# Row maxima of the grouped-query heads: both heads of a block side by side in the two halves of the array's rows

## Chip, core and metric

One core of a Trainium2 chip runs the whole program. The metric is the device time of one execution in microseconds (us). TensorE is PE in the rows (its weight loads are PEld), VectorE is DVE, ScalarE is ACT, GpSimd is POOL, and SyncE, which issues the transfers, is SP.

## The reference, cut to what matters

A trunk of two layers over 1024 latent tokens and 256 context tokens. Layer 0 has two kinds of attention over 1280 keys: differential attention, and grouped-query attention with 8 query heads of 64 columns, four to each of 2 key heads. The change touches only the second kind:

```python
def gqa_attention(q, k, v):
    q = q.reshape(bsz, nq, B_KV_HEADS, B_REP, HEAD_DIM)
    s = jnp.einsum('bqgrd,bkgd->bgrqk', q, k) * (HEAD_DIM ** -0.5)
    p = jax.nn.softmax(s.astype(jnp.float32), axis=-1).astype(v.dtype)
    o = jnp.einsum('bgrqk,bkgd->bqgrd', p, v)
```

The softmax stays the same whatever is subtracted from the scores of a query, so long as the exponentials stay in range. The kernel subtracts the largest score over the keys, found ahead of time.

## The kernel before

The kernel is built with a tile framework: the program issues operations in its own order, a scheduler orders them on each engine by its own costs and by priorities (`tc.high_priority`), and each engine then runs its list strictly in that order.

The class `Grouped` handles the grouped heads after the differential ones. The work is cut into 8 blocks `j`, each with 512 queries of two heads (`s` = 0 and 1). `prepare` brings the queries of a block to 64 rows of head dimension. Each float32 value is split into a rounded high part and the rest, the low part. For head `s` the tile `q[s]` holds the high part in rows 64s to 64s+63 and the low part in the other 64 rows. The keys lie in three groups of 512, 512 and 256 (`GROUPS`); `k1` holds the keys' high part twice, in both halves of the rows.

Per block there are ten steps `kt`, one for each 128 keys. In a step `exponentials` computes the scores of 128 keys by 512 queries for either head, with two matmuls that add up in one PSUM bank (L1433, L1434), and ACT writes the exponential to `pt` (L1435). POOL or DVE adds `pt` to a running sum (L1439). Two steps later `values` multiplies `pt` by the values (L1448). The values of one head are 64 columns wide, so that the two heads use the two halves of the array's columns: `tile_position=(0, s * 64)`. These are two instructions, one for each half of the columns. `divide` (L1463 to L1470) does the normalisation of a block.

The shift of the next block is found at the same time. In each of the steps 0 to 7, `ahead` calls `maximum` for 128 queries of one head: three matmuls of all 128 rows (L1407, into three banks), one DVE maximum of each bank (L1409), and one more of the three results (L1410), whose negative goes to `w`. At step 8 `shifts` turns `w` around (L1416) and puts it into the tile `q2`, which the matmul L1434 applies. `first` does the same for block 0, during the last steps of the differential attention (L1324 and L1202 are its values and its transposes there).

All these scores, for exponentials and for maxima, come from one pool of five PSUM banks (`bank`).

Of the kernel before, what the change touches and what calls it, by code (L numbers as in the profile page):

```python
# [9 lines left out]
F32 = mybir.dt.float32  # L10
# [3 lines left out]
AX = mybir.AxisListType  # L14
PSUM = bass.MemoryType.PSUM

P = 128
# [38 lines left out]
class Trunk:  # L56
# [838 lines left out]
    def merged(self, w, bs, k0, mod, gcol, step):  # L895
# [88 lines left out]
        for n in range(2):  # L984
            ahead(n)
        yield
        for n in range(len(seq)):
            if n + 2 < len(seq):
                ahead(n + 2)
            x, p = seq[n]  # L990
            on = x in (6, 7, 4, 3)
            if p == 0:
                ps[x] = ps[{6: 1, 7: 6, 4: 7, 3: 5}[x]] if on else [self.ps() for _ in range(4)]
            if p == 6 and x in (1, 6, 7, 4):
                for j in range(4):
                    jj, h = {1: (j, 0), 6: (j, 1), 7: (4 + j, 1), 4: (4 + j, 0)}[x]
                    self.tc.keep_in_program_order(self.residual(jj, self.acc[jj, h]))
            a, b = parts.pop((x, p)), bparts.pop((x, p))
            for j in range(4):
                f = slice(j * P, (j + 1) * P)  # L1000
                self.mm3(ps[x][j], a[0][:, f], a[1][:, f], *b, p == 0 and not on, p == pairs[-1], skip_group_check=on)
            if p == pairs[-1]:
                with self.tc.high_priority(offset=60):
                    plus(x)
            step(x, p)
# [33 lines left out]
    def conv(self):  # L1039
# [49 lines left out]
        for h in range(2):  # L1089
            if h == 1:  # L1090
                parts = self.blocks([self.cw_in[17], self.cw_in[1]])
            for i, x in enumerate((8, 16, 0, 9)):
                first(x, h)
                if h == 1:
                    if x == 16:
                        z[0, "y"] = convolve(0, [z[8, i] for i in range(2)])
                        y = z[0, "y"]
                        times(y[0], z[0, 0], y[0])
                        self.leave(y[0], 0, 0)
                    self.combine(i)  # L1100
# [243 lines left out]
class Grouped:  # L1344
# [52 lines left out]
            nc.vector.scalar_tensor_tensor(out=q[s][o, :], in0=tr[r, :], scalar=0.125,  # L1397
                                           in1=q[s][r, :].bitcast(F32), op0=ALU.mult, op1=ALU.subtract)

    def maximum(self, j, i, s):  # L1400

        nc = self.nc
        c = 64 - s * 64
        mx = self.at.pl.tile([P, 4], F32, name="mx3", bufs=4)
        for g, ((g0, gn), (k1, _)) in enumerate(zip(GROUPS, self.k[j // 4])):
            o = self.bank()
            nc.tensor.matmul(o[:, 0:gn * P], lhsT=self.q[j][s][:, i * P:(i + 1) * P], rhs=k1[:, 0:gn * P], start=True,  # L1407
                             stop=True)
            nc.vector.reduce_max(out=mx[:, g:g + 1], in_=o[:, 0:gn * P], axis=AX.X)  # L1409
        nc.vector.reduce_max(out=self.w[j % 2][:, i, c:c + 1], in_=mx[:, 0:3], axis=AX.X, negate=True)  # L1410

    def shifts(self, j):
        nc = self.nc
# [57 lines left out]

    def first(self, k):
        with self.t.tc.high_priority(offset=60):
            for m in range(k * 4, min(8, k * 4 + 4)):
                self.maximum(0, m // 2, m % 2)
            if k == 1:
                self.shifts(0)
        if k == 1:
            self.prepare(1)
# [18 lines left out]

    def ahead(self, j, m):
        with self.t.tc.high_priority(offset=40):  # L1500
            if m < 8:
                self.maximum(j, m // 2, m % 2)
            if m == 8:
                self.shifts(j)

# [57 lines left out]
```

## Time and profile before

| | |
|---|---|
| median of 3 runs (lowest to highest) | 2538.68 us (2537.96 to 2540.46) |
| profiled execution, its own time | 2539.14 us |
| its span from the first instruction to the last | 2537.3 us |
| granted TensorE clock, mean | 0.989 of full speed |
| share of the span in which PE, DVE, ACT, POOL are busy | 96%, 73%, 48%, 12% |

The time of the profiled execution is 1.8 us above its span and 0.5 us above the median. The grouped heads lie between 511 and 751 us of the span, the maxima of block 0 between 494 and 511 us.

### The profile page before, as it was taken

What the parts mean: (1) busy time and instruction counts of PE and PEld (TensorE: products, weight loads), DVE (VectorE), ACT (ScalarE), POOL (GpSimd) and SP (SyncE); (2) the same over time, 40 slices, a digit from 0 to 9 for tenths busy, and PEclk for the clock granted to TensorE, in tenths of its full rate; (3) what the DMA queues carried; (4) which work ended last, traced back from release to release, by engine and by line L of the source; (5) the groups of instructions that cost most, each with busy time, mean ns of one, the idle gap of its engine ahead of it and who ended that gap; (6) DMA issues with size and microseconds to landing.
All of it is one profiled execution on the core that took longest, in us unless ns stands there. A gap on an engine that the chain in (4) does not pass through costs nothing.

```text
span 2537.3 us, 30356 instructions
## 1 busy us (share of the span) xinstructions
PE 2437.0 (96%) x11070; PEld 1902.7 (75%) x11070; DVE 1861.5 (73%) x2903; ACT 1226.4 (48%) x1986; POOL 297.5 (12%) x201
## 2 busy tenths in 40 slices
PE   7999899999999999999999998999999999999997
PEld 5888677744448778777788877887877888878886
DVE  4857888887867887776857688766788556585766
ACT  3113578755552465444444446533246555545443
POOL 0001000044440420000000033001131000000011
PEclk9999999999999999999999999999999999999999
DMA  7811111000011047778642320223203444853231
GB/s 271 282 61 51 22 23 46 7 25 6 1 65 68 1 154 239 254 252 302 242 150 92 109 89 31 68 76 127 92 30 105 163 142 152 295 186 133 100 108 67
DMA packets 118519, 297.15 MB, mean 117 GB/s; under 512 B 13536, under 2 KB 19296, under 8 KB 118368
## 3 DMA queue, kind: packets, MB, share of 16 engines
q1 hardware_dynamic: 118368, 295.20, 34.2%
q8 instruction: 87, 1.43, 0.2%
q14 instruction: 64, 0.52, 0.1%
HBM read 225.29 MB, written 63.96 MB: 114 GB/s over the span
## 4 chain that ended last, share of the span: by engine, by line
PE 65%; DVE 19%; ACT 6%; DMA 6%; issue 3%; SPq 0%; POOL 0%; ACTq 0%; DVEq 0%; POOLq 0%
PE ps L75 17%; PE ps L74 17%; PE ps L76 17%; PE pv L1448 3%; DMA raw<-in_w 3%; PE one L1324 2%; PE s L1433 2%; DVE acc L675 1%; PE s L1407 1%; PE s L1434 1%; PE s L1187 1%; DMA xr<-in_xT 1%; ACT e L1193 1%; DVE mx L1409 1%; DVE a L79 1%
## 5 line engine op out<-in xcount | busy, mean ns | idle before, releaser
L74 PE MATMUL ps<-bh,part 128*128 128x512 f32 x784 | 306.7, 392 | 7.7 <-ACT part L940 7.5
L75 PE MATMUL ps<-bl,part 128*128 128x512 f32 x784 | 305.1, 390 | 0.0
L76 PE MATMUL ps<-bh,part 128*128 128x512 f32 x784 | 303.3, 391 | 0.0
L940 ACT CAST part<-a 128x512 fp32r<-128x512 f32 x196 | 121.5, 622 | 270.7 <-PE ps L75 129.8
L74 PE MATMUL ps<-T,a 128*128 128x512 f32 x608 | 240.5, 396 | 10.3 <-ACT tmp L882 4.1
L75 PE MATMUL ps<-T,a 128*128 128x512 f32 x608 | 238.5, 392 | 1.6 <-DVE T L79 1.6
L76 PE MATMUL ps<-T,a 128*128 128x512 f32 x608 | 238.0, 392 | 0.0
L79 DVE TENSOR_TENSOR part<-a,part 128x512 fp32r<-128x512 f32 x196 | 135.1, 691 | 130.6 <-ACT part L940 129.9
L79 DVE TENSOR_TENSOR a<-raw,a 128x1024 fp32r<-128x1024 f32 (+1 forms) x114 | 121.6, 1068 | 98.8 <-PE ps L75 68.4
L79 POOL TENSOR_TENSOR hid<-graw,hid 128x512 fp32r<-128x512 f32 x24 | 38.0, 1607 | 1258.1 <-ACT hid L538 1258.0
L74 PEld LDWEIGHTS ps<-bh,part 128*128 128x128 f32 x784 | 147.1, 188 | 42.9 <-ACT part L940 13.0
L74 PE MATMUL ps<-H,a 128*128 128x512 f32 x456 | 177.8, 390 | 0.0
L75 PE MATMUL ps<-H,a 128*128 128x512 f32 x456 | 177.6, 389 | 0.0
L76 PE MATMUL ps<-H,a 128*128 128x512 f32 x456 | 177.3, 389 | 0.0
L76 PEld LDWEIGHTS ps<-bh,part 128*128 128x128 f32 x784 | 147.1, 188 | 33.2 <-DVE part L79 2.6
L75 PEld LDWEIGHTS ps<-bl,part 128*128 128x128 f32 x784 | 147.1, 188 | 30.1 <-DVE bl L79 0.4
L538 ACT CAST a<-raw 128x1024 fp32r<-128x1024 f32 (+1 forms) x114 | 101.4, 906 | 136.0 <-PE ps L75 78.5
L858 DVE TENSOR_TENSOR tmp<-ps,tmp 128x512 f32<-128x512 f32 x114 | 78.5, 688 | 109.7 <-PE ps L76 73.5
L74 PEld LDWEIGHTS ps<-T,a 128*128 128x128 f32 x608 | 114.6, 188 | 42.9 <-ACT tmp L882 7.6
L79 DVE TENSOR_TENSOR bl<-b,bh 128x1024 fp32r<-128x1024 f32 x98 | 119.9, 1223 | 22.3 <-ACT bh L927 22.0
L75 PEld LDWEIGHTS ps<-T,a 128*128 128x128 f32 x608 | 114.7, 189 | 25.9 <-DVE T L79 2.9
L76 PEld LDWEIGHTS ps<-T,a 128*128 128x128 f32 x608 | 114.9, 189 | 24.1
(417 smaller groups left out, 5864.8 us busy)
## 6 DMA issues: line engine op xcount, KB each, us to landing
gq<-tmp SPq DMA_DIRECT2D x196, 256.0 KB, 3.3
b<-gq SPq DMA_DIRECT2D x98, 512.0 KB, 3.2
raw<-in_w SPq DMA_DIRECT2D x72, 512.0 KB, 4.5
a<-in_w SPq DMA_DIRECT2D x140, 256.0 KB, 5.6
raw<-in_adaT SPq DMA_DIRECT2D x48, 512.0 KB, 5.9
adar<-in_adaT SPq DMA_DIRECT2D x32, 512.0 KB, 5.0
raw<-in_cw_in SPq DMA_DIRECT2D x24, 512.0 KB, 3.7
ada<-in_adaN SPq DMA_DIRECT2D x16, 512.0 KB, 8.4
```

The lines of the kernel that those rows point to most:

```text
L74: mm(ps, lhsT=lh, rhs=rh, start=start, stop=False, **kw)
L75: mm(ps, lhsT=lh, rhs=rl, start=False, stop=False, **kw)
L76: mm(ps, lhsT=ll, rhs=rh, start=False, stop=stop, **kw)
L79: return eng.tensor_tensor(out=out, in0=a, in1=hi.bitcast(F32), op=ALU.subtract)
L538: self.nc.scalar.copy(out=hi, in_=src)
L675: self.eng(L("mul")[j]).tensor_tensor(out=acc, in0=acc, in1=y, op=ALU.mult)
L858: nc.vector.tensor_tensor(out=o, in0=a, in1=b, op=op)
L940: self.tc.keep_in_program_order(nc.scalar.copy(out=hi, in_=src))
L1187: nc.tensor.matmul(o, lhsT=q[:, c], rhs=k1[:, 0:gn * P], start=True, stop=False)
L1324: nc.tensor.matmul(pv[:, 0:256], lhsT=t.vA[kt][:, h * P:(h + 1) * P], rhs=self.pt[kt // 4][:, kt % 4, :], start=kt == 0, stop=kt == KT - 1)
L1433: nc.tensor.matmul(o, lhsT=k1[:, c], rhs=self.q[j][s], start=True, stop=False)
L1448: nc.tensor.matmul(self.pv[j][s * 64:(s + 1) * 64, :], lhsT=t.vB[:, kt, g * 64:(g + 1) * 64], rhs=pt[:, s, :], start=kt == 0, stop=kt == K ...
```

## The change

`maximum` handles both heads of 128 queries in one call. For each group of keys it takes two banks and issues two matmuls: head 0 with rows 0 to 63 of the array, head 1 with rows 64 to 127 (`tile_position=(s * 64, 0)`). Each multiplies the high part of the queries by the high part of the keys; the product of the queries' low part, which the matmul of 128 rows contained, is left out of the maximum. The scores that are exponentiated are as before. Six DVE maxima of the banks follow as before, and one final maximum for both heads in place of two. A call is made in the steps 0, 2, 4 and 6, where there was one in each of the steps 0 to 7.

```diff
-    def maximum(self, j, i, s):
-        nc = self.nc
-        c = 64 - s * 64
-        mx = self.at.pl.tile([P, 4], F32, name="mx3", bufs=4)
+    def maximum(self, j, i):
+        nc = self.nc
+        mx = self.at.pl.tile([P, 2, 3], F32, name="mx3", bufs=4)
         for g, ((g0, gn), (k1, _)) in enumerate(zip(GROUPS, self.k[j // 4])):
-            o = self.bank()
-            nc.tensor.matmul(o[:, 0:gn * P], lhsT=self.q[j][s][:, i * P:(i + 1) * P], rhs=k1[:, 0:gn * P], start=True,
-                             stop=True)
-            nc.vector.reduce_max(out=mx[:, g:g + 1], in_=o[:, 0:gn * P], axis=AX.X)
-        nc.vector.reduce_max(out=self.w[j % 2][:, i, c:c + 1], in_=mx[:, 0:3], axis=AX.X, negate=True)
+            os = [self.bank()[:, 0:gn * P] for s in range(2)]
+            for s, o in enumerate(os):
+                r = slice(s * 64, s * 64 + 64)
+                nc.tensor.matmul(o, lhsT=self.q[j][s][r, i * P:(i + 1) * P], rhs=k1[r, 0:gn * P], start=True, stop=True,
+                                 tile_position=(s * 64, 0))
+            for s, o in enumerate(os):
+                nc.vector.reduce_max(out=mx[:, 1 - s, g:g + 1], in_=o, axis=AX.X)
+        w = self.w[j % 2][:, i, :].rearrange("p (s c) -> p s c", s=2)[:, :, 0]
+        nc.vector.reduce_max(out=w, in_=mx, axis=AX.X, negate=True)
...
-            if m < 8:
-                self.maximum(j, m // 2, m % 2)
+            if m < 8 and m % 2 == 0:
+                self.maximum(j, m // 2)
```

The scheduler orders the engines anew, and the line numbers behind the edit grow by 4 (L1433, L1434 and L1448 are L1437, L1438 and L1452 there, L1407 is L1409, L1409 is L1412). Of PE's list before this is one step of the second block (j = 1), with a maximum of the next block in it (`k_...` and `q_...` are tiles of keys and queries):

```order
L1433 MATMUL s<-q_4875,k_4535 128x512
L1434 MATMUL s<-q_4877,k_4536 128x512
L1433 MATMUL s<-q_4876,k_4535 128x512
L1407 MATMUL s<-k_4535,q_5064 128x512
L1407 MATMUL s<-k_4546,q_5064 128x512
L1407 MATMUL s<-k_4557,q_5064 128x256
L1434 MATMUL s<-q_4878,k_4536 128x512
L1448 MATMUL pv<-pt,vB 64x512 x2
```

And these are rows of one step of the fifth block (j = 4) in PE's list of the change, again with a maximum of the next block:

```order
L1437 MATMUL s<-q_5559,k_5538 128x512
L1409 MATMUL s<-k_5527,q_5793 128x512
L1409 MATMUL s<-k_5527,q_5794 128x512
L1409 MATMUL s<-k_5538,q_5793 128x512
L1409 MATMUL s<-k_5538,q_5794 128x512
L1438 MATMUL s<-q_5561,k_5539 128x512
L1452 MATMUL pv<-pt,vB 64x512
L1409 MATMUL s<-k_5549,q_5793 128x256
L1409 MATMUL s<-k_5549,q_5794 128x256
L1452 MATMUL pv<-pt,vB 64x512
```

The last pair of maxima now stands between the two instructions of `values`, which stood together. Over the whole list, from the first score matmul of block 0 on, the instructions of `values` stood in 63 runs of two, 28 of one and one of six; now they stand in 46 runs of two, 62 of one and one of six. The maxima stood in 58 runs; now they stand in 65. In 47 of 56 pairs of 512 columns and 21 of 28 pairs of 256 columns the second matmul follows the first directly. Counted with `divide`'s matmuls, the list changed from whole-array matmuls to column halves 92 times and back 91 times. Now it changes into column halves 109 times (75 from the whole array, 34 from row halves), out of them to the whole array 81 times, and from or to row halves otherwise 96 times (38 whole to rows, 31 rows to whole, 27 columns to rows).

The maxima of block 0 stand between matmuls of the differential attention. Before, PE's list went there as follows:

```order
L1407 MATMUL s<-k_4535,q_4567 128x512
L1407 MATMUL s<-k_4546,q_4567 128x512
L1324 MATMUL one<-pt,vA 128x256
L1202 MATMUL one<-ident,e 128x128 x2
L1407 MATMUL s<-k_4557,q_4567 128x256
L1324 MATMUL one<-pt,vA 128x256
```

Now the pairs are torn by matmuls of the whole array:

```order
L1409 MATMUL s<-k_4546,q_4566 128x512
L1324 MATMUL one<-pt,vA 128x256
L1202 MATMUL one<-ident,e 128x128 x4
L1409 MATMUL s<-k_4546,q_4567 128x512
L1409 MATMUL s<-k_4557,q_4566 128x256
L1324 MATMUL one<-pt,vA 128x256
```

There 5 of 8 pairs of 512 columns and none of the 4 pairs of 256 columns stay together, and the list changes into row halves 14 times and out of them 14 times.

## Rows read from the trace of the kernel before

**Rows 1.** The page's head: span, then each engine's busy time and instructions.

```profile
span 2537.3 us, 30356 instructions
PE 2437.0 (96%) x11070; PEld 1902.7 (75%) x11070; DVE 1861.5 (73%) x2903; ACT 1226.4 (48%) x1986; POOL 297.5 (12%) x201
```

**Rows 2.** Busy time by stretch: the grouped heads, then block 0's maxima.

```profile
core 0: us, PE busy (x) PEld busy (x) DVE busy (x) ACT busy (x) POOL busy (x), PEclk, DMA share, GB/s
510.70:751.20 240.50, 237.08 (x915) 113.15 (x913) 183.19 (x311) 129.81 (x228) 117.39 (x51) 1.00 0.04 11
494.30:510.70 16.40, 16.36 (x86) 12.87 (x84) 15.72 (x37) 6.83 (x14) 0.00 (x0) 1.00 0.05 6
```

**Rows 3.** Timeline of one step: start, length, engine, line, operation, count.

```profile
574.70 0.50 PE L1433 MATMUL s<-q,k 128*128 128x512 f32 x1
575.03 0.39 PE L1434 MATMUL s<-q,k 128*128 128x512 f32 x1
575.26 0.40 PE L1433 MATMUL s<-q,k 128*128 128x512 f32 x1
575.50 0.74 PE L1407 MATMUL s<-k,q 128*128 128x512 f32 x3
575.52 0.60 ACT L1435 ACTIVATE pt<-s 128x512 f32<-128x512 f32 x1 [1.11 <-PE s L1434]
575.93 1.62 DVE L1409 TENSOR_REDUCE mx<-s 128x1 f32<-128x512 f32 x3 [0.78 <-PE s L1407]
576.08 0.39 PE L1434 MATMUL s<-q,k 128*128 128x512 f32 x1
576.40 0.20 PEld L1448 LDWEIGHTS pv<-pt,vB 128*64 128x64 f32 x4 [0.24 <-issue]
576.40 1.08 PE L1448 MATMUL pv<-pt,vB 128*64 128x512 f32 x4
577.41 0.50 PE L1433 MATMUL s<-q,k 128*128 128x512 f32 x1
```

**Rows 4.** Timeline of PE: lone instructions of L1448, a run of six, transposes.

```profile
521.54 1.07 PE L1448 MATMUL pv<-pt,vB 128*64 128x512 f32 x2
522.55 0.61 PE L1407 MATMUL s<-k,q 128*128 128x512 f32 x2
523.09 1.07 PE L1448 MATMUL pv<-pt,vB 128*64 128x512 f32 x2
524.09 0.50 PE L1433 MATMUL s<-q,k 128*128 128x512 f32 x1
...
565.49 0.49 PE L1416 MATMUL one<-ident,w 128*128 128x128 f32 x3
565.82 0.49 PE L1392 MATMUL one<-ident,qB 128*128 128x128 f32 x3
...
723.55 1.07 PE L1448 MATMUL pv<-pt,vB 128*64 128x512 f32 x2
724.55 0.50 PE L1433 MATMUL s<-q,k 128*128 128x512 f32 x1
...
747.91 2.80 PE L1448 MATMUL pv<-pt,vB 128*64 128x512 f32 x12
750.53 1.03 PE L1463 MATMUL one<-e,ones 128*64 128x512 f32 x4
```

**Rows 5.** Groups by line and shape, 510.7 to 751.2 us: busy, mean ns, idle before.

```profile
L1448 PE MATMUL pv<-pt,vB 128*64 128x512 f32 x320 | 100.8, 617 | 0.4 <-ACT pt L1435 0.4
L1409 DVE TENSOR_REDUCE mx<-s 128x1 f32<-128x512 f32 x112 | 72.7, 684 | 35.7 <-PE s L1407 35.6
L1407 PEld LDWEIGHTS s<-k,q 128*128 128x128 f32 x168 | 31.1, 188 | 13.0 <-ACT pt L1435 2.4 <-DVE mx L1409 1.3 <-DVE y L473 0.8
L1409 DVE TENSOR_REDUCE mx<-s 128x1 f32<-128x256 f32 x56 | 23.2, 414 | 0.0
L1448 PEld LDWEIGHTS pv<-pt,vB 128*64 128x64 f32 x320 | 18.6, 135 | 27.6 <-issue 24.4 <-ACT pt L1435 2.2 <-ACT ot L1456 0.4
L1410 DVE TENSOR_REDUCE w<-mx 128x1 f32<-128x3 f32 x56 | 8.4, 149 | 0.8
```

More of the change, by code (lines that the diff above doesn't have):

```diff
@@ L1473, in first @@
         with self.t.tc.high_priority(offset=60):
-            for m in range(k * 4, min(8, k * 4 + 4)):
-                self.maximum(0, m // 2, m % 2)
+            for i in range(k * 2, min(4, k * 2 + 2)):
+                self.maximum(0, i)
             if k == 1:
```

## The prediction

> **What bounds the kernel now.** The page's head comes first: PE is busy for 96% of the span, DVE for 73% [rows 1]. The busy times by stretch come next, because the change touches one stage. Between 510.7 and 751.2 us, where the grouped heads run, PE is busy 237.1 of 240.5 us at full clock and DVE 183.2 [rows 2]: PE sets this stage, and DVE waits 35.6 us for the maxima's matmuls alone [rows 5]. Between 494.3 and 510.7 us, where block 0's maxima stand, DVE is nearly as full as PE, 15.7 to 16.4 of 16.4 us [rows 2].
>
> A matmul's own length is no price, since matmuls overlap; what counts is the distance from one start to the next. The timeline of a step gives it [rows 3]: the score matmuls L1434 and L1433 start 0.23 us apart, and three maxima take 576.08 - 575.50 = 0.58 us, which is 0.232 for each of 512 columns and 0.115 for that of 256. The step is 2.71 us long (577.41 - 574.70).
>
> The same rows show what the column halves of `values` cost. Each of its instructions leaves two records, so that "x4" is both halves. Their four weight loads lie within 0.20 us where one takes 0.135 [rows 3, 5]: the halves run at the same time. The pair takes 1.01 us from its start to the next score matmul [rows 3]. A lone half takes 1.01 or 1.00 us as well (522.55 - 521.54, 724.55 - 723.55; 28 stand alone in the stage) [rows 4]. So a half without its partner costs a whole pair. In the run of six, three pairs take 2.62 us [rows 4], 0.87 each, and the other 0.14 of a single run is its first weight load (0.05) and the end of the run (0.10), where nothing overlaps.
>
> Changes between modes show beside it [rows 3]. The last matmul ahead of `values` occupies 0.32 us where others take 0.23; the first one behind occupies 0.33. I put going into column halves at 0.15 us (0.09 in front, 0.05 for the load) and going out at 0.20 (0.10 at the end of the run, 0.10 for the load of the next matmul's 128 columns).
>
> To see whether these prices are complete I add them up over the list of the kernel before: 320 score matmuls at 0.232 (74.2), 112 and 56 maxima (32.4), 94 runs or parts of runs of `values` at 0.865 (81.3), 8 of `divide` (7.0), 69 transposes at 0.11 (7.6; rows 4: three in 0.33), two others (1.7), 92 changes at 0.15 and 91 at 0.20 (32.0). This makes 236 us of the 240.5 measured; some 4 are waits.
>
> **The change, part by part, between 511 and 751 us.**
>
> *Maxima.* If two matmuls in different row halves run at the same time as the column halves do, a pair costs what one cost. 47 of 56 wide pairs and 21 of 28 narrow ones stand together: 47 + 18 streams of 0.232 and 21 + 14 of 0.115 make 19.1 us in place of 32.4. That is -13.3. No row of the trace has row halves: the bounds are -13.3 and 0 (no overlap at all). I take -13.3, as the column halves are the nearest row.
>
> *`values`.* 92 runs (63 + 28 + 1) become 109 (46 + 62 + 1), and the streams, three in the run of six, 94 become 111. That is 17 more streams at 0.865: +14.7.
>
> *Changes of mode.* Before 92 x 0.15 + 91 x 0.20 = 32.0. After 109 x 0.15 into column halves and (81 + 38 + 31 + 27) x 0.20 for all others: 51.8. That is +19.8. The bounds for those that touch row halves are 0 and the column price. With 0 only the 17 added runs of column halves count, 17 x 0.35 = 6.0. I take the column price, the only one measured. The Trainium skill, page "TensorEngine Tiling (Array Packing)", section "Tiling Modes", says that a change of the tiling mode, not merely of the tile, drains the engine. The trace agrees for column halves (0.32 and 0.33 us against 0.23); no row here shows row halves. By the page this term is +19.8; by the rows without it, 6.0 to 19.8.
>
> *Banks.* A call took three of the five banks, now it takes six within a step, so some matmuls of a call wait for a bank that the same step still uses. The nearest row: an exponential ends at 576.12, 1.09 us after its L1434 started (575.03) [rows 3]. In the new order the fourth maximum could start some 0.9 us after that L1434 (0.23 to the second L1433, 0.33 with the change, one pair, the weight load). That is 0.2 us of waiting for each of 28 calls, about 6. The bounds are 0 (the scheduler placed another bank there) and 14 (a wait of a DVE maximum, 0.68 us [rows 5], not wholly covered: 0.5 per call). Behind a waiting maximum stands everything on PE, the next L1438 and `values` first.
>
> *DVE.* 56 final maxima of 0.149 us become 28 of about the same length: -4.2 us on an engine with 57 us of slack. Worth nothing here; the cover is the PE list itself. The 168 maxima of banks stay.
>
> **Block 0, 494 to 511 us.** On PE: 16 x 0.232 + 8 x 0.115 = 4.6 becomes 11 x 0.232 + 8 x 0.115 = 3.5 (-1.1), and 28 changes at 0.20 add 5.6. That is +4.5 for PE, in a stretch that DVE paces nearly as closely: bounds 0 and 4.5, I take 2.
>
> **Sum.** -13.3 + 14.7 + 19.8 + 6 + 2 = +29.2 us. The profiled execution took 2539.14 us, so it gives 2568.3. The median lies 0.46 below that execution, so I predict 2568. The stages behind run on the same lists as before and merely move.
>
> **The rivals.**
>
> *The row halves don't overlap.* Then the 73 pairs that stand together give nothing: 47 x 0.232 + 21 x 0.115 + 5 x 0.232 = 14.5 more, 2582 us. For it: nothing in the trace shows row halves. Against it: column halves do overlap.
>
> The Trainium skill, page "TensorE: Matmul & The Clock Gate", section on packing small matmuls by row and column tiling, gives 3.07 times for four row tiles. No run here shows that yet; it speaks against this rival.
>
> *Changes to and from row halves are free.* Then that term is 6.0 and not 19.8: 2554 us. Against it stand the three prices of column halves in one step.
>
> *The banks bind.* Waits at their upper bounds, 14 and 4.5, add 10.5: 2578 us. For it: in the trace PE hardly ever waits for a bank with three maxima to a step; with six of five banks it has no spare one.
>
> *Faster.* The one mechanism that ends there: a row run of maxima in a gap of `values` costs `values` nothing, since the second half joins the first across it, and the row halves don't drain. 25 gaps hold maxima alone. Without them there are 84 runs against 92 and 92 streams against 94: -8 x 0.35 - 2 x 0.865 - 13.3 - 1.1 = -19, 2520 us. It turns faster from the point where streams and changes together add less than the 14.4 us that the pairs save. Against it: in the trace of before two lone halves with two maxima between take 2.55 us (524.09 - 521.54) where a pair takes 1.01, so a gap of 0.54 costs one whole further run [rows 4].
>
> **How the numbers follow.** I give the forecast 0.45, the rows without overlap 0.2, free row changes 0.14, the banks 0.12, the faster case 0.06, and 0.03 to nothing in particular, near no change. The range 2548 to 2590 takes in the forecast, the two slower rivals with some waits on top, and the free changes with fewer waits; outside it remain about 2 in 10. A difference of less than 0.2% (5 us) can't be told from no change here. So faster 0.07, same 0.04, slower 0.89.
>
> **What the profile after would show.** PE should stay busy above 97% between 511 us and the end of the stage, which should end near 780 us. The matmuls L1409 of one pair should start within a few hundredths of a microsecond or at most one weight load (0.1 us) of each other. Lone L1452 should again take 1.00 us, some 62 times. The matmul ahead of a run of L1409 should occupy 0.32 us and the one behind it 0.33. DVE's busy time in the stage should fall by 4 us. PE's waits for DVE or ACT should add up to 5 to 10 us more. The prediction would be wrong if lone halves were cheaper than 0.9 us beside row halves, if pairs started 0.23 us apart, or if PE idled for tens of microseconds for banks.

## The result and the profile after

The change takes 2576.54 us (median of 4 runs, 2572.97 to 2577.40) against 2538.32 us for the kernel before on the same chip (2537.36 to 2540.46): a ratio of 1.0144, 95% interval 1.0132 to 1.0156. It is 38 us slower. The forecast was 2568, in a range of 2548 to 2590.

The page's head of the change, to set beside [rows 1]:

```profile
span 2575.0 us, 30326 instructions
PE 2470.1 (96%) x11070; PEld 1896.5 (74%) x11070; DVE 1860.9 (72%) x2871; ACT 1223.6 (48%) x1986; POOL 296.3 (12%) x201
```

The span grew by 37.7 us. The number of matmuls is the same, and their half-array form was meant to save time, but PE is busy for 33 us more. The busy times by stretch show where; these are block 0's maxima and then the grouped heads of the change, the stretches that answer to [rows 2]:

```profile
core 0: us, PE busy (x) PEld busy (x) DVE busy (x) ACT busy (x) POOL busy (x), PEclk, DMA share, GB/s
494.30:514.80 20.50, 20.50 (x88) 12.22 (x86) 16.16 (x33) 7.38 (x14) 0.00 (x0) 1.00 0.01 5
514.80:789.30 274.50, 265.93 (x917) 106.68 (x916) 181.15 (x283) 126.84 (x229) 116.26 (x51) 0.99 0.03 10
```

The stage of the grouped heads took 240.5 us and takes 274.5, 34 more. The stretch ahead of it is 4 us longer (16.4 before). Together that is the whole difference.

One maximum of the change, in PE's timeline; the step before is in [rows 3]:

```profile
602.06 0.40 PE L1437 MATMUL s<-q,k 128*128 128x512 f32 x1
602.39 1.08 PE L1409 MATMUL s<-k,q 64*128 64x512 f32 x4
603.40 0.50 PE L1438 MATMUL s<-q,k 128*128 128x512 f32 x1
603.83 0.38 PE L1409 MATMUL s<-k,q 64*128 64x256 f32 x1
604.14 1.07 PE L1452 MATMUL pv<-pt,vB 128*64 128x512 f32 x2
605.15 0.38 PE L1409 MATMUL s<-k,q 64*128 64x256 f32 x1
```

Each price can be read here. The matmul ahead of the row halves occupies 0.33 us (602.39 - 602.06) and not 0.23. Four wide row-half matmuls take 1.01 us, where four of the whole array would take 0.93. A lone narrow one takes 0.31, where it took 0.115. A single score matmul between two runs of row halves takes 0.43. The lone half of `values` takes 1.01, as before.

The pairs do run at the same time. At 613.41 us, where both banks of a narrow pair had come free, two matmuls together cover 0.39 us, as long as a lone one (0.38 above), and the next matmul starts 0.32 us behind them, against 0.31 behind a lone one:

```profile
609.84 2.37 POOL L1443 TENSOR_TENSOR e<-e,pt 128x1024 f32<-128x1024 f32 x1 [2.82 <-ACT pt L1439]
609.97 2.79 DVE L1473 SCALAR_TENSOR_TENSOR r<-ra,r 128x512 f32<-128x512 f32 x1
610.37 1.02 PE L1409 MATMUL s<-k,q 64*128 64x512 f32 x4
610.89 0.18 PEld L1409 LDWEIGHTS s<-k,q 64*128 64x128 f32 x1 [0.23 <-ACT pt L1439]
611.32 0.51 PE L1438 MATMUL s<-q,k 128*128 128x512 f32 x1
611.75 1.07 PE L1452 MATMUL pv<-pt,vB 128*64 128x512 f32 x2
612.68 3.13 DVE L1412 TENSOR_REDUCE mx<-s 128x1 f32<-128x512 f32 x6
613.41 0.39 PE L1409 MATMUL s<-k,q 64*128 64x256 f32 x2 [0.59 <-DVE mx L1412]
613.73 1.07 PE L1452 MATMUL pv<-pt,vB 128*64 128x512 f32 x2
```

The same rows show the wait for a bank. DVE is held by the division L1473 until 612.68, then does the six maxima; the narrow pair waits on PE for the first of these to free a bank, 0.59 us, and the second half of `values` waits behind it. Such a wait, of 0.49 to 0.65 us, comes back once in each of the six blocks behind the first. The rows show a second kind of wait: the weight load of the fourth wide matmul (610.89) waits for the exponential (ACT) that frees its bank, so that this matmul cannot run beside the third one.

The list of waits for PE has one entry that matters, 510 to 785 us:

```profile
engine line waited for: us in total, times, longest us
PE s L1409 <- DVE mx L1412: 7.2, 7, 3.8
```

In the kernel before the same entry was 0.3 us. The longest of the seven ends at 536.9 us. Busy times around it, of the change:

```profile
531.00:537.00 6.00, 2.24 (x11) 0.66 (x8) 5.96 (x6) 0.76 (x2) 4.63 (x2) 0.85 0.00 0
537.00:541.00 4.00, 3.98 (x9) 1.43 (x10) 3.04 (x7) 0.60 (x1) 0.00 (x0) 0.50 0.00 0
541.00:546.00 5.00, 5.00 (x19) 2.53 (x18) 2.82 (x5) 1.79 (x3) 3.35 (x2) 0.89 0.00 0
```

PE is busy for 2.2 of 6 us. The granted clock falls within this stretch (0.85 on its mean), is 0.50, that is 1.2 GHz, through the whole of the next 4 us, and returns to 2.4 GHz within the 5 us behind (0.89). So the wait is paid twice: 3.8 us of idle time and, as an estimate from these shares, some 5 us of work at half clock, which cost about 2.5 us more.

### The profile page after: what moved, and what is told of

It reads as the page before. It is cut to its first block, busy times and chain, and to the rows that moved or that the text cites. A ratio compares the mean times of both kernels' runs of the same rounds, so it can differ in the third digit from the quotient of the medians.

```text
span 2575.0 us, 30326 instructions
## 1 busy us (share of the span) xinstructions
PE 2470.1 (96%) x11070; PEld 1896.5 (74%) x11070; DVE 1860.9 (72%) x2871; ACT 1223.6 (48%) x1986; POOL 296.3 (12%) x201
## 4 chain that ended last, share of the span: by engine, by line
PE 67%; DVE 18%; ACT 7%; DMA 4%; issue 3%; POOL 0%; SPq 0%; ACTq 0%; DVEq 0%; POOLq 0%
PE ps L75 17%; PE ps L74 17%; PE ps L76 17%; PE pv L1452 4%; DMA raw<-in_w 3%; PE one L1324 2%; PE s L1437 2%; PE s L1409 1%; PE s L1438 1%; DVE acc L675 1%; DVE a L79 1%; PE s L1187 1%; ACT e L1193 1%; PE one L1202 1%; PE s L1188 1%
## 5 line engine op out<-in xcount | busy, mean ns | idle before, releaser
L74 PEld LDWEIGHTS ps<-T,a 128*128 128x128 f32 x608 | 114.5, 188 | 42.1 <-DVE tmp L858 6.4
L1412 DVE TENSOR_REDUCE mx<-s 128x1 f32<-128x512 f32 (+1 forms) x192 | 102.0, 594 | 50.7 <-PE s L1409 50.4
L1439 ACT ACTIVATE pt<-s 128x512 f32<-128x512 f32 x160 | 90.6, 595 | 100.9 <-PE s L1438 96.3
```

Source lines behind the costliest of these rows:

```text
L74: mm(ps, lhsT=lh, rhs=rh, start=start, stop=False, **kw)
L1412: nc.vector.reduce_max(out=mx[:, 1 - s, g:g + 1], in_=o, axis=AX.X)
L1439: nc.scalar.activation(pt[:, s, :], o, AF.Exp)
```

## The experiments

All are compared with the kernel before, run beside them on the same chip. Runs of different sets are compared by their ratios to it.

### First set: one part at a time

**Pairs without row halves.** The change, with the matmuls of all 128 rows put back:

```diff
-                r = slice(s * 64, s * 64 + 64)
-                nc.tensor.matmul(o, lhsT=self.q[j][s][r, i * P:(i + 1) * P], rhs=k1[r, 0:gn * P], start=True, stop=True,
-                                 tile_position=(s * 64, 0))
+                nc.tensor.matmul(o, lhsT=self.q[j][s][:, i * P:(i + 1) * P], rhs=k1[:, 0:gn * P], start=True, stop=True)
```

> Pairs, bursts of six banks and the one final maximum as in the change, but the matmuls of the maxima use all 128 rows again, so there are no row halves. PE's list has 61 lone halves of `values` and 111 streams, as in the change. Theory 1 (lone halves, changes of mode and bank waits cost the time; what row halves save by overlapping they give back in changes of mode): the prices add up to 256.6 us for the stage against 257.4 for the change, and block 0 loses its 28 changes, so 2568 to 2580 us, within 0.4% of the change. Theory 2 (the row halves themselves are what costs): about 2545 us. Theory 3 (free row changes, the pairs gain 14 us): slower than the change by some 14 us, 2590.

2572.91 us against 2540.57 (ratio 1.0128, 1.0113 to 1.0143). Without a single row half nearly the whole loss is still there. So the row halves as such are not what costs 38 us, and they don't save 14 either: the torn list is what the two kernels have in common.

**The change with the halves of `values` glued.** The second half is given priority as soon as the first is issued:

```diff
         for s in range(2):
-            nc.tensor.matmul(self.pv[j][s * 64:(s + 1) * 64, :], lhsT=t.vB[:, kt, g * 64:(g + 1) * 64], rhs=pt[:, s, :],
-                             start=kt == 0, stop=kt == KT - 1, tile_position=(0, s * 64))
+            with t.tc.high_priority(offset=200 * s):
+                nc.tensor.matmul(self.pv[j][s * 64:(s + 1) * 64, :], lhsT=t.vB[:, kt, g * 64:(g + 1) * 64],
+                                 rhs=pt[:, s, :], start=kt == 0, stop=kt == KT - 1, tile_position=(0, s * 64))
```

> The change, with the second half of `values` given priority, so that it stands directly behind the first: 77 runs of two and one of six, 80 streams, 48.8 us of mode changes by the prices. Theory 1: the sum falls from 257.4 to 227.4 us; minus 20 to 34 us against the change, 2542 to 2557 us. Rival (the halves are torn only where PE would have waited for a bank anyway, so that gluing moves the wait): less than 8 us gained, 2568 us or more.

2565.35 us (1.0097, 1.0082 to 1.0112): 12 us faster than the change by the two ratios, between the two theories. Its busy times show where the rest went; these are three places of the glued change:

```profile
574.00:580.00 6.00, 5.95 (x19) 2.76 (x19) 4.10 (x10) 2.09 (x4) 1.61 (x1) 0.72 0.00 0
672.00:678.00 6.00, 4.63 (x15) 2.28 (x15) 4.60 (x9) 1.10 (x3) 2.60 (x2) 0.72 0.01 3
704.00:712.00 8.00, 6.63 (x24) 3.29 (x23) 6.61 (x9) 1.91 (x4) 4.61 (x2) 0.79 0.01 2
```

PE's waits for the DVE maxima rose from 7.2 to 10.3 us, and at these places the granted clock fell, which it did not at the corresponding steps of the change. A lone half was partly cover: without it PE stands at the bank sooner. My theory that tearing alone explained the halves' price was too simple; tearing and the burst hang together.

**Row halves alone, one head per call.** The kernel before, with only the form of the matmul changed:

```diff
-            nc.tensor.matmul(o[:, 0:gn * P], lhsT=self.q[j][s][:, i * P:(i + 1) * P], rhs=k1[:, 0:gn * P], start=True,
-                             stop=True)
+            r = slice(s * 64, s * 64 + 64)
+            nc.tensor.matmul(o[:, 0:gn * P], lhsT=self.q[j][s][r, i * P:(i + 1) * P], rhs=k1[r, 0:gn * P], start=True,
+                             stop=True, tile_position=(s * 64, 0))
```

> The kernel before, with one head per call as there, but each matmul of a maximum uses only the high parts, in its half of the rows, and nothing overlaps on purpose. 63 runs of maxima change into row halves and out; 92 streams of `values`; by the prices 256.1 us for the stage against 236.3. Theory 1 (a change to or from row halves costs what one to column halves costs): plus 17 to 26 us against before, 2555 to 2565 us. Rival (changes of row halves free): 2530 to 2540 us.

2558.54 us (1.0069, 1.0054 to 1.0084), 18 us slower. Here the matmuls of a call all use the same half of the rows and run one behind the other, and `values` is torn no more than before (92 streams, before 94), so this is the price of the mode by itself. A step of it in PE's timeline (L1434 and L1435 are the score matmuls here, L1408 the maxima, L1449 `values`):

```profile
600.28 0.40 PE L1434 MATMUL s<-q,k 128*128 128x512 f32 x1
600.60 0.84 PE L1408 MATMUL s<-k,q 64*128 64x512 f32 x3
601.38 0.50 PE L1435 MATMUL s<-q,k 128*128 128x512 f32 x1
601.81 1.08 PE L1449 MATMUL pv<-pt,vB 128*64 128x512 f32 x4
```

Beside [rows 3]: 0.32 us in place of 0.23 ahead of the three maxima, 0.78 in place of 0.58 for them, 0.43 in place of 0.32 for the score matmul behind. That is 0.40 us for one run of row halves, which is one change in and one out: 0.20 each, as the prediction had taken it over from the column halves.

**The kernel before with the halves of `values` glued**, the same edit as above on the kernel before.

> The kernel before with only the halves of `values` glued by priority: 81 streams for 94, 159 changes for 183, the sum 220.8 us against 236.3. Theory 1: minus 11 to 17 us against before, 2521 to 2528 us. Rival (the lone halves stand where PE waits anyway): within 5 us of before.

2531.16 us (0.9964, 0.9949 to 0.9978): 9 us faster than the kernel before, a little less than the 11 to 17 expected and more than the rival allows. The 28 lone halves of the kernel before cost time too.

### Second set: no burst, and a better place for the row halves

**Calls cut in two.** Four banks in the even steps, two in the odd ones:

```diff
-            if m < 8 and m % 2 == 0:
-                self.maximum(j, m // 2)
+            if m < 8:
+                self.maximum(j, m // 2, ((0, 1), (2,))[m % 2])
```

> The change with its call cut in two: in the even steps the two wide pairs (four banks), in the odd steps the narrow pair (two banks) and the final maximum. No priority is changed. The halves of `values` come apart 10 times in place of 62, 85 streams; the changes of mode stay dear (53.1 us by the prices); the sum is 235.2 us against 236.3 for the kernel before and 257.4 for the change. Theory 1 (the burst of six tiles on five banks tears `values` and makes PE wait; row halves alone only break even): between 5 us faster and 8 us slower than before, with PE's waits near those of before. Rival (row halves as such cost the 35 us): 20 us or more slower than before.

2551.61 us (1.0049, 1.0032 to 1.0067), 9 us slower than the kernel before by the medians and 12 by the ratio, outside the range that I gave. But of the 38 us some 24 are gone with this edit alone, and the rival (20 or more) falls. Its single executions spread from 2548.68 to 2560.75, so the last few microseconds are not to be read into.

**Late row halves.** Calls cut in two, `values` glued, block 0 in the whole array, and the second score matmul ahead of the maxima:

```diff
-            nc.tensor.matmul(o, lhsT=k2[:, c], rhs=self.q2[j][s], start=False, stop=True)
+            with self.t.tc.high_priority(offset=200):
+                nc.tensor.matmul(o, lhsT=k2[:, c], rhs=self.q2[j][s], start=False, stop=True)
...
-                self.maximum(0, i)
+                self.maximum(0, i, rows=False)
```

> As the spread calls, `values` glued, block 0 in the whole array, and the second score matmuls of a step go ahead of the maxima, so that a run of row halves stands directly ahead of `values` and the array goes from the whole to rows to columns and back (52 changes from rows to columns): three changes in place of four. The sum is 217.8 us against 236.3. Theory 1: 8 to 18 us faster than before, the upper end if the waits stay at those of before. Rival (changes between rows and columns cost more than one of the others): no faster than 5 us.

2528.90 us (0.9948, 0.9930 to 0.9966): 13.5 us faster than the kernel before, as expected. Most of this is not the row halves' work: the kernel before with nothing but its halves glued had reached 0.9964.

**The same with narrow groups in the whole array** (`if rows and g < 2`).

> As the run with late row halves, but the narrow groups of 256 columns use the whole array, one matmul per head with both parts of the queries; only the wide pairs use row halves. About 30 runs of row halves fewer, 22 narrow streams more: some 3 us less than with all in row halves. Theory 1: 10 to 22 us faster than before and 2 to 6 us faster than the run with all groups in row halves. Rival (a run of row halves costs no more than a run in the whole array): slower than that run by 2 to 3 us.

2531.96 us (0.9961, 0.9948 to 0.9974). Faster than before as expected, but the 2 to 6 us that I expected against all groups in row halves did not come. It is 3 us slower by the medians, which the two intervals do not separate; in the traces the stage takes 228.9 us here and 227.9 with all groups in row halves. So row halves for the narrow groups cost nothing here, where I had expected a loss; why, this run does not show.

**Spread pairs, glued, all in the whole array**, neither late nor in row halves.

> Both heads per call and one final maximum as in the change, calls cut in two, `values` glued, but all maxima in the whole array with 128 rows: no row halves at all. The sum is 219.3 us (80 streams, 192.2, and 27.1 for changes) against 236.3 before and 256.6 for the same matmuls in bursts of six. Theory 1: 8 to 17 us faster than before, level with the best of the row halves within 5 us. Rival (the pairs in row halves save what they seem to, 13 us): 10 us or more slower than the run with late row halves.

2536.64 us (0.9982, 0.9972 to 0.9992): 6 us faster, where 8 to 17 were expected, and 8 us slower than late row halves, between the 5 of the one theory and the 10 of the other. Neither held. Which of the two differences, the place or the row halves, made these 8 us, this run can't say; the third set can.

### Third set: the burst and the row halves, each by itself

**Late row halves with the call whole**, six banks in one step:

```diff
-            if m < 8:
-                self.maximum(j, m // 2, ((0, 1), (2,))[m % 2])
+            if m < 8 and m % 2 == 0:
+                self.maximum(j, m // 2)
```

> The run with late row halves, but with the call of the change whole: all three pairs of a call, six banks of five, in one step. The prices make the same sum (218.0 us against 217.8), so the difference to that run is the price of the burst: PE's waits for banks and what they bring with them. Theory 1: 8 to 20 us slower than late row halves with the call cut in two, with waits for the maxima and second score matmuls in PE's rows. Rival (the burst only tears `values`; once these are glued it costs nothing): within 4 us.

**Late, but all in the whole array**, and **the late row halves once more** on the same chip:

> The run with late row halves, with all maxima in the whole array, 128 rows, everything else alike: what row halves themselves are worth in the best place found for them. The sum is 219.3 us against 217.8. Theory 1 (given back in changes of mode): within 4 us of late row halves. Rival (the earlier run of spread pairs in the whole array was 8 us slower because row halves do gain): 6 to 12 us slower.

> The kernel of the late row halves once more, on the same chip as the two runs that differ from it in one thing each: 8 to 18 us faster than before, as it was.

The three medians are 2544.85 (1.0021, 1.0009 to 1.0034), 2530.93 (0.9961, 0.9948 to 0.9974) and 2525.93 us (0.9941, 0.9924 to 0.9957), with the kernel before at 2539.36.

The burst costs 19 us although `values` is whole in both lists. In the groups by line and shape, first the kernel with bursts (511 to 758 us), then that without (512 to 740), where L1414 are the maxima's matmuls, L1420 their DVE maxima, L1447 and L1449 the score matmuls and L1464 is `values`:

```profile
L1414 PE MATMUL s<-k,q 64*128 64x256 f32 x56 | 21.0, 383 | 10.7 <-DVE mx L1420 10.7
```

```profile
L1414 PE MATMUL s<-k,q 64*128 64x256 f32 x56 | 14.2, 382 | 0.3 <-DVE mx L1420 0.2
```

The last number is PE's idle time ahead of the narrow maxima: 10.7 us of waiting for a bank against 0.3. PE's timeline of the kernel with bursts shows a second part, which is not listed as idle:

```profile
628.36 0.39 PE L1449 MATMUL s<-q,k 128*128 128x512 f32 x1
628.68 1.16 PE L1414 MATMUL s<-k,q 64*128 64x512 f32 x5
629.77 1.08 PE L1464 MATMUL pv<-pt,vB 128*64 128x512 f32 x4
631.58 0.38 PE L1414 MATMUL s<-k,q 64*128 64x256 f32 x1 [0.73 <-DVE mx L1420]
```

Four wide matmuls and one narrow one take 1.09 us there. And this is a step of the kernel without bursts:

```profile
606.57 0.39 PE L1449 MATMUL s<-q,k 128*128 128x512 f32 x1
606.89 0.85 PE L1414 MATMUL s<-k,q 64*128 64x512 f32 x4
607.67 1.08 PE L1464 MATMUL pv<-pt,vB 128*64 128x512 f32 x4
608.68 0.50 PE L1447 MATMUL s<-q,k 128*128 128x512 f32 x1
```

The four wide ones take 0.78 us, where four of the whole array take 0.93, and the halves of `values` stand together behind them.

A third part is the clock. Two of the waits of the kernel with bursts are 4.0 and 3.3 us long, and around them the granted clock falls, where the kernel without bursts has 1.00 through the whole stage:

```profile
530.00:545.00 15.00, 11.77 (x43) 6.52 (x45) 11.58 (x18) 5.25 (x10) 6.77 (x3) 0.77 0.00 1
720.00:750.00 30.00, 26.69 (x94) 11.15 (x92) 14.49 (x15) 13.63 (x25) 15.19 (x8) 0.89 0.00 1
```

By the medians the row halves by themselves are worth 5 us (2530.93 against 2525.93), between the 4 that I had allowed and the 6 to 12 of the rival. The traces show that less than half of this is theirs. These are the stages from the first score matmul to the last of `divide`: all in the whole array, late row halves, and the earlier run of late row halves, which is the same kernel:

```profile
512.80:742.50 229.70, 224.50 (x916) 110.62 (x914) 180.42 (x285) 124.03 (x228) 119.31 (x51) 1.00 0.04 12
511.30:739.20 227.90, 224.66 (x916) 100.10 (x915) 177.69 (x284) 124.11 (x228) 119.18 (x51) 1.00 0.04 12
512.10:740.00 227.90, 224.65 (x916) 100.03 (x914) 177.67 (x285) 124.07 (x228) 119.14 (x51) 1.00 0.04 12
```

The stage gains 1.8 us; the other 3 lie ahead of it and behind it, where the programs are the same. The two runs of one kernel differ as much there: their spans are 2525.8 and 2530.7 us with the same stage. So the row halves do gain, by about 2 us of the stage, less than 0.1% of the time, where the runs are long, the banks are free, and the list goes from rows to columns anyway; 5 us is not shown. That is what theory 1 said (within 4 us), and the rival falls. The other difference, the place, is worth some 5 us by the ratios of the two runs with all in the whole array (0.9982 and 0.9961). But the kernel before with glued halves stands at 0.9964 as well, so against that kernel calls for both heads in the late place gain nothing.

## Why the prediction was right, step by step

The direction, the place and the mechanisms were right; the size was 8.5 us short, 29.2 in place of 37.7 us of the span. The prices read in the trace after are those of the forecast, so the direction was not luck.

*Maxima, -13.3.* That the pairs overlap showed in the trace. The rival without overlap falls. But many pairs don't get the whole of it, because the second of a pair waits for its bank. Of the 47 wide pairs that stand together 20 started 0.18 to 0.34 us apart, and 19 runs of four wide ones took 0.95 to 1.01 us, not two streams with load and end, 0.66. Most of that loss belongs to the banks, below; without bursts such a run takes 0.78 us.

*`values`, +14.7.* The lone half costs a whole run, as forecast: 1.01 us in the trace after. Gluing gave 9 us in the kernel before and 12 in the change, so the price is real, but not all of it came back, since a lone half also covered bank waits.

*Changes of mode, +19.8.* Row halves pay what column halves pay: the matmul in front occupies 0.33 us and not 0.23, and the one behind 0.43, because it mostly stands ahead of the next change too. The run with row halves alone settles it, 18 us for 63 runs and block 0. The rival of free changes falls; it would have been faster than or level with the kernel before. The Trainium skill, page "TensorEngine Tiling (Array Packing)", section "Tiling Modes", says that a change of the tiling mode drains the engine. The trace after agrees for row halves (0.33 us against 0.23).

*Banks, +6.* This is the step that was sized too low. I took 0.2 us for each of 28 calls, and for the upper bound 14. The stage grew by 34.0 us; without the three terms on the list (21.2) 12.8 remain for waits. That lies below my bound of 14, but is twice what I took. I had looked at one bank and one exponential. What I left out is that DVE is at times busy elsewhere: with `divide` once per block (0.49 to 0.65 us of PE idle each time) and with three vector operations of the differential attention's last normalisation (`rsqrt0`, L471 to L473), which made the one wait of 3.8 us and, with it, the half clock. That the burst is dear is shown apart from all else by the run with late bursts, 19 us.

*Block 0, +2.* The stretch grew by 4 us, of which one lies ahead of the first maximum (it starts at 495.4 us, before at 494.3); my upper bound was 4.5. PE is busy through all of the 20.5 us, so DVE did not cover the changes of mode as I thought.

*DVE.* The final maxima fell from 56 of 0.149 us to 28, and DVE's busy time in the stage from 183.2 to 181.2. It brought nothing, as forecast.

Of what was to show it, some points held: the matmul ahead of row halves occupies 0.33 us, a lone half of `values` takes 1.00 us each of the 56 times that it stands alone (six more of the 62 in the list share their time with a matmul of `divide`), and PE's idle time in the stage grew by 5.2 us (from 240.5 - 237.1 to 274.5 - 265.9). Others failed: PE was not busy above 97% in the whole stage (265.9 of 274.5 is 96.9%), the stage ended at 789 us and not near 780, DVE's busy time fell by 2 us and not by 4, the matmul behind a run mostly occupies 0.43 us, and the 20 pairs named above started too far apart. That last was one of the signs of being wrong, and it is the bank term that it speaks against.

How the 12.8 us divide can be estimated from the trace after. PE's idle time accounts for 5.2, the half clock for about 2.5, and the 19 runs of four wide maxima, at about 0.3 us each above 0.66, for 6. That is 1 us too much, which the prices leave open. So the exponentials, for which I had taken 6, cost at most what I had taken (0.1 us of each run is there without bursts too), and the waits for DVE with the half clock came on top.

## What to carry to other kernels

Before half-array matmuls are put into a list, count the changes of mode that they bring: here a run of row halves cost 0.40 us between whole-array matmuls, and a wide pair saves 0.23, so a run must be two wide pairs long to break even, or stand directly beside a run that changes the mode anyway (the second follows from the prices; no run tried it by itself). Two matmuls that share the array by halves are only cheap together, so they should be tied in the list; nothing but a priority for the second was needed, and it made the kernel before faster by 0.36%. A call that takes more PSUM banks at once than the pool has makes the list depend on how soon other engines free them, even where these are idle on average. The best version here, with all three taken care of, is 0.5 to 0.6% faster than the kernel before (0.9948 and 0.9941) and so beats both. But the priority alone brings 0.36%, and the form that the change was about brings 1.8 us, less than 0.1%: measure a change against the best list without it, and in the stage that it touches.

## What the runs showed of the hardware

A DVE operation can take several times its usual length while POOL works. In the timeline of DVE and POOL of the change:

```profile
530.82 4.89 POOL L1443 TENSOR_TENSOR e<-e,pt 128x1024 f32<-128x1024 f32 x2 [0.37 <-ACT pt L1439]
531.03 2.48 DVE L472 TENSOR_SCALAR sq<-sq 128x512 f32<-128x512 f32 x1
533.55 2.71 DVE L473 TENSOR_TENSOR y<-y,sq 128x512 f32<-128x512 f32 x1
```

In the kernel before, the first of the same L472 took 0.43 us, with POOL idle:

```profile
513.29 0.43 DVE L472 TENSOR_SCALAR sq<-sq 128x512 f32<-128x512 f32 x1
```

L472 and L473 of the change, 2.48 and 2.71 us, made the longest wait of PE. The division behind the shorter waits has the same mark: L1473 took 2.79 us beside POOL at 609.97, and L1474 of the change took 0.68 us with POOL idle and 2.75 us beside it:

```profile
722.41 0.68 DVE L1474 SCALAR_TENSOR_TENSOR ot<-ot,r 128x512 f32<-128x512 f32 x1
...
751.55 2.57 POOL L1443 TENSOR_TENSOR e<-e,pt 128x1024 f32<-128x1024 f32 x1 [2.78 <-ACT pt L1439]
751.92 2.75 DVE L1474 SCALAR_TENSOR_TENSOR ot<-ot,r 128x512 f32<-128x512 f32 x1
```

That the one causes the other was not tried here.

PE's granted clock went to half speed (1.2 GHz) around an idle time of 3.8 us and stayed there through the next 4 us, in which PE was busy for 3.98. This wait on PE thus cost more than its own length. In the glued change shorter waits were followed by it too. This one ends at 574.05, and between 574 and 580 us the granted clock is 0.72 on the mean, as shown above:

```profile
574.05 0.38 PE L1409 MATMUL s<-k,q 64*128 64x256 f32 x1 [1.40 <-DVE mx L1412]
```

Behind another wait of this length, 1.45 us until 641.03, it stayed at 1.00.
